# VectorE side work dealt out by kind of projection tile, and the key norm first in each RWKV pair, in a decoder step of retention and RWKV-7

## The chip, the cores and the metric

The kernel runs on one core of one Trainium2 chip. The metric is device time in microseconds (us) of one execution. The kernel before was timed three times. Engines are named as in the profile: PE is TensorE, PEld its weight loads, DVE is VectorE, ACT is ScalarE, POOL is GpSimd, SP is SyncE, which issues most of the transfers. SPq is SP's issuing queue. HBM is the chip's memory.

## The reference

One step of a hybrid decoder on 512 prompt rows and 8 sampled rows of 1024 values. One normalised input goes through one combined projection `w_in`. Branch A is retention (4 heads, keys of 256, values of 512), branch B is RWKV-7 (16 heads of 64). Each is gated, normalised and projected down; both are merged, projected out, and followed by an embedding gate and a last norm.

```
P = rmsnorm(x) @ w_in
q, k, v, g_a, sh, g_b, m_a, m_b = split(P)
# branch A, per head, chunks of 128 rows
inner = (q k^T) * dmask;  o = inner v + (q * q_dec) S;  S = chunk_dec * S + (k * k_dec)^T v
y_a = rmsnorm(o) * silu(g_a)
# branch B, per head of 64; z = sh mixed with the row before
w = decay(w0 + tanh(wl) @ w2);  a = sigmoid(a0 + al @ a2)
kk = k * k_k / |k * k_k|
S = S * w - (S kk) (a * kk)^T + v k'^T;  o_t = S r_t
y_b = groupnorm(o) * silu(g_b)
out = x + (sigmoid(m_a) * (y_a @ w_down_a) + sigmoid(m_b) * (y_b @ w_down_b)) @ w_out, ...
```

The 8 sampled rows take one step from stored states of both branches.

## The kernel before

**Products.** Nearly all work on PE is a *tile*: 128 columns of a weight against the 520 rows (512 and 8), in two halves of 256 and 264 rows (`HV`). A product of 32-bit values is three passes, high by high, high by low and low by high, so that a half is 24 matmuls (`mm_half`, L154). `weights` fetches a tile's weights on SP's queue (`raw`, 512 KB), ACT copies the high part (`whi`, L141), and DVE subtracts it to get the low part (`wlo`, L142). There are two buffers of `whi` and of `wlo`, so that PE waits for a `wlo` that comes late. The second of three passes, the one that reads `wlo`, comes early in each half.

**Order.** The Tile framework puts each engine's instructions into an order of its own, from the program's order, its dependences and durations that it assumes, before anything runs. Each engine then works through its list strictly in turn: an instruction that waits holds up all that stands behind it on that engine. `tc.issue_after` keeps what it encloses behind a given instruction. Reordering the program's text thus moves instructions on all engines.

**Stages.** First the input, its norm and transposes, and the shifted key tiles (to 120 us). Then come 8 RWKV pairs (to some 262 us): each is a generator `pair` that the loop at L556 to L575 steps through, with the projection tiles of two pairs further on (`filler`) between its steps. Then come four retention heads (L735 to L861, from 262 to 740 us). The RWKV chunks follow (740 to 945 us), then the last projections.

**In a pair.** Two pairs are under way at a time: the first two steps of one stand just ahead of the `g` products of the pair before it. The first step makes the low-rank products on PE (`pw`, L440 and L441: two halves for the decay, two for `a`), which ACT takes out of PSUM with a tanh (`sg` and `a`, L442); DVE sums them up (`cum`, L445) and ACT raises them (`Pm`, `iP`). The second step makes the key norm (`pn`, L457, two halves), which DVE takes out by `kkn` (L458), and then `KRS`, `b1`, `BK`, `km` on DVE. Later steps make the 16 products `g` (L498), which DVE masks (`GM`, L504); DVE's rescaling `BK` (L518); PE's transposes of `BK` (L523), that ACT takes out (`BKT`, L524); transposes of the values and the bonus `pb`. All of `pw`, `pn`, `g`, the transposes and `pb` take turns in three PSUM banks (`bank()`, tag "x"); one more bank takes the fourth `g`. The projections' halves have four banks of their own.

**In a head.** Key and query tiles with their rotation (`rope`: two tiles each; on DVE the products L751 to L753, the second of which goes to a buffer `s_` of which there is one), four value tiles, scores (`sc`, L787), the values' transposes (`vt`, L800; ACT takes `vhi`, DVE `vlo` L802), the sampled rows (`sampled`, L690), four gate tiles (`gs`, L823, ACT with Silu), in heads 2 and 3 also four tiles of branch B's gate (L828, O_GB), the outputs `o` (L838), their norms (`rsqrt`, chains of small DVE operations L172 to L180), the new states `st` (L849, through the buffer `s_` and a store on POOL's queue), the transposes `ot` and the products with the gates `gs` (L858).

**Side work.** DVE also has work that PE doesn't wait for until the chunks: `solve` (L608), 62 steps of two dependent operations on a buffer `M` (L614 and L616; 8 stores to `TTd` at the end), and `rwkv_sampled` (L634), 4 times 9 operations on a state that is loaded into the same buffer `M` when the stores have read it. `beside` (L663) strings both together with a pause between. `advance` (L671) deals them out: it adds a share of `WORK` to `due` and issues steps until what they cost (elements and 60 for each) has used it up. It is called behind each key, query, value and gate tile, 12 times in a head, always with the share 1/42; the pause is worth two shares.

Of the kernel before, what the change touches and what calls it, by code (L numbers as in the profile page):

```python
# [8 lines left out]
F32 = mybir.dt.float32  # L9
# [3 lines left out]
ALU = mybir.AluOpType  # L13
# [4 lines left out]
T, B8, NT = 512, 8, 520  # L18
HT = 256
D = 1024  # L20
KT = 8
# [3 lines left out]
H = 4  # L25
# [7 lines left out]
V_MU, V_W0, V_A0, V_KK, V_KA, V_RK, V_LW, V_LB, V_PG = 0, 25, 33, 41, 49, 57, 65, 73, 81  # L33
# [46 lines left out]
def body(tc, A, O, dbg=None, upto="Z"):  # L80
# [3 lines left out]
    act, dve, pe, sp, pool = nc.scalar, nc.vector, nc.tensor, nc.sync, nc.gpsimd  # L84
# [7 lines left out]
    with es:  # L92
# [15 lines left out]
        def bank(name="x", tag="x"):  # L108
            return px.tile([128, 512], F32, tag=tag, name=name)
# [18 lines left out]
        HV = ((0, 0, HT), (1, HT, NT))  # L128
# [33 lines left out]
        def proj(src, rhi, rlo, **kw):  # L162
            return mm([(*weights(src), 0, KT)], rhi, rlo, **kw)
# [33 lines left out]
        vcol = lambda o, i: vec[:, o + i:o + i + 1]  # L197
# [7 lines left out]
        def gate(c_, m, dst, fn, scale=1.0):  # L205
            g = gp.tile([128, NT], F32, tag="mg", name="mg", bufs=2)
            for (j, c0, c1), ps in zip(HV, proj(w_in[:, col(c_, m)], hhi, hlo)):
                act.activation(g[:, c0:c1], ps, fn, scale=scale)
            sp.dma_start(dst[m], g)
# [114 lines left out]
        pA = pA_.__enter__()  # L324
# [55 lines left out]
        zk = []  # L380
        pss = [bank("pss") for _ in range(2)]
        for p in range(NPAIR):
# [14 lines left out]
            if p == 2:  # L397
                gb = pA.tile([128, D], F32, tag="GM", name="gb")
# [18 lines left out]
        rns = pA.tile([128, NT], F32R, tag="zwa", name="rns", bufs=1)  # L417
# [6 lines left out]
        inh = pA.tile([128, NPAIR, 128], F32R, tag="inh", name="inh", bufs=1)  # L424
# [7 lines left out]
        SPL = 2  # L432
        def pair(p, zr, zv):
            cs = slice(p * 128, (p + 1) * 128)
            sg = pA.tile([128, NT], F32, tag="sgt", name="sg")
            a = pA.tile([128, NT], F32, tag="a", name="a")
            for dst, bi, u, w, wl in ((sg, p, W[0], Z[0], ZL[0]), (a, 8 + p, W[1], Z[1], ZL[1])):
# [13 lines left out]
            act.activation(iP, cum[:, 0:T], AF.Exp, scale=0.5 * E05)  # L451
            dve.tensor_copy(PC[:, p, :], Pm[:, :, C])
            yield
            kkn = pA.tile([128, NT], F32, tag="kkn", name="kkn")
            for j, c0, c1 in HV:
                pn = bank("pn")[:, 0:c1 - c0]
                pe.matmul(pn, inh[:, p, :], rns[:, c0:c1], start=True, stop=True)  # L457
                dve.scalar_tensor_tensor(kkn[:, c0:c1], zk[p][:, c0:c1], vcol(V_KK, p), pn, ALU.mult, ALU.mult)  # L458
            KRS = pA.tile([128, NCH, 128], F32, tag="KRS", name="KRS")
            k4 = KRS.rearrange("p (c e) (f t) -> p c (e f) t", e=2, f=2)  # L460
            P0 = Pm.rearrange("p (c e) t -> p c e t", e=2)
# [43 lines left out]
            for hh in range(2):  # L505
                hs_ = slice(64 * hh, 64 * hh + 64)
                GM = GMs[hh]
                h = 2 * p + hh
# [100 lines left out]
        def solve():  # L609
            for s in range(1, C - 1):  # L610
                n = C - 1 - s
                tm = pB.tile([128, 1024], F32, tag="tm", name="tm", bufs=1)
                tv = tm[:, 0:s * n].rearrange("p (i t) -> p i t", t=n)
                dve.tensor_tensor(tv, M[:, 0:s, s:s + 1].to_broadcast([128, s, n]),  # L614
                                  M[:, s:s + 1, s + 1:C].to_broadcast([128, s, n]), ALU.mult)
                dve.tensor_tensor(M[:, 0:s, s + 1:C], M[:, 0:s, s + 1:C], tv, ALU.add)  # L616
                yield s * n
            dve.memset(M.rearrange("p s t -> p (s t)")[:, 0::C + 1], 1.0)
            for c in range(NCH):
                sp.dma_start(TTd[c].rearrange("t h u -> h t u"), M[c * 16:(c + 1) * 16])  # L620
            yield 0
# [40 lines left out]

        def beside():  # L663
            yield from solve()
            yield 2 * WORK / 42
            yield from rwkv_sampled()

        extra = beside()
        due, WORK = 0.0, sum(s * (C - 1 - s) + 60 for s in range(1, C - 1)) + 36 * (HQ * C / 2 + 60)

        def advance(share=1.0 / 42):  # L671

            nonlocal due
            due += share * WORK
            with tc.issue_after(marks[1]):
                while due > 0:
                    w_ = next(extra, None)
                    if w_ is None:
                        break
                    due -= w_ + 60  # L680
# [54 lines left out]
        for h in range(H):  # L735
            roped = {}

            def rope(nm, c_):
                xx = rp.tile([128, 2, NT], F32, tag="rx", name="rx")
                for i in range(2):  # L740
                    x = xx[:, i, :]
                    for (j, c0, c1), ps in zip(HV, proj(w_in[:, col(c_, i)], hhi, hlo)):
                        act.activation(x[:, c0:c1], ps, AF.Copy)
                    advance()
                hi = pB.tile([128, 2, T], F32R, tag=nm + "hi", name=nm + "hi")
                lo = pB.tile([128, 2, T], F32R, tag=nm + "lo", name=nm + "lo")
                res = []
                for i, (u, w, op) in enumerate(((xx[:, 0], xx[:, 1], ALU.subtract), (xx[:, 1], xx[:, 0], ALU.add))):
                    m1 = pB.tile([128, NT], F32, tag=f"ro_{nm}", name="m1", bufs=2)
                    m2 = pB.tile([128, NT], F32, tag="s_", name="m2", bufs=1)  # L750
                    dve.tensor_tensor(m1, u, cos, ALU.mult)  # L751
                    dve.tensor_tensor(m2, w, sin, ALU.mult)
                    dve.tensor_tensor(m1, m1, m2, op)  # L753
                    act.activation(hi[:, i, :], m1[:, 0:T], AF.Copy)
                    dve.tensor_tensor(lo[:, i, :], m1[:, 0:T], hi[:, i, :], ALU.subtract)
                    act.activation((qs if nm == "q" else ks)[:, h, i, :], m1[:, T:NT], AF.Copy, scale=1.0 if nm == "q" else 1 / 16.0)
                    res.append(m1)
                roped[nm] = (hi, lo, res)

            def values():  # L760
                for i in range(4):
                    x = pB.tile([128, NT], F32, tag="vg", name="vT", bufs=4)
                    for (j, c0, c1), ps in zip(HV, proj(w_in[:, col(O_V + DV * h, i)], hhi, hlo)):
                        act.activation(x[:, c0:c1], ps, AF.Copy)
                    vT.append(x)
                    advance()

            vT = []
            if False:
# [12 lines left out]
            for jt in range(4):  # L782
# [3 lines left out]
                for x, (i, a_, b_) in enumerate(seq):  # L786
                    pe.matmul(ps[:, 0:n], a_[:, i, 128 * jt:128 * jt + 128], b_[:, i, 128 * jt:T],  # L787
                              start=(x == 0), stop=(x == 5))
# [31 lines left out]
            for i in range(4):  # L820
                g = pB.tile([128, NT], F32, tag="vg", name="gs", bufs=4)
                for (j, c0, c1), ps in zip(HV, proj(w_in[:, col(O_GA + DV * h, i)], hhi, hlo)):
                    act.activation(g[:, c0:c1], ps, AF.Silu)  # L823
                act.activation(gs8[:, 4 * h + i, :], g[:, T:NT], AF.Copy)
                gs.append(g)
                advance()
            for m in range(GBC[h], GBC[h + 1]):
                gate(O_GB, m, GBd, AF.Silu)  # L828

            oss = pB.tile([128, 4], F32, tag="oss", name="oss", bufs=2)  # L830
            ort = pB.tile([128, 4], F32, tag="ort", name="ort", bufs=2)
# [26 lines left out]
                dve.tensor_tensor(y, ps, y, ALU.mult)  # L858
                sp.dma_start(YAd[4 * h + i], y)
            sampled_out(h, po)  # L860
        advance(1.0)  # L861
        pR_.__exit__(None, None, None)
        pB_.__exit__(None, None, None)
        rp_.__exit__(None, None, None)
# [323 lines left out]
        for x in HV:  # L1188
            j = x[0]
# [48 lines left out]
```

## Time and profile before

| what | value |
|---|---|
| runs of the kernel before | 1121.35, 1121.46, 1123.13 us; median 1121.46 |
| the profiled execution | 1122.57 us |
| its span | 1120.8 us |
| its mean granted TensorE clock | 0.976 of full |
| PE busy | 1066.7 us, 95% of the span |
| DVE, ACT, POOL busy | 786.1, 508.1 and 63.0 us |
| read from HBM, written | 139.28 and 61.58 MB |
| chain that ended last | PE 79%, DMA 10%, DVE 6%, ACT 3% |

The span is what the profiler saw from the first to the last instruction; the execution's own time is 1.8 us longer. A busy share is an average over stages. Where one engine is busy nearly all the time, its idle stretches show what the others could give back, and each idle stretch is listed with the instruction that ended it. The granted clock is in shares of full speed: 1.00 is 2.4 GHz, 0.50 is 1.2 GHz.

### The profile page before, as it was taken

The page shows a single profiled execution, that of the slowest core. Times are in us where ns is not written, and L with a number is a line of the kernel's source. Part 1 is how long each engine was busy: PE and PEld are TensorE (multiplying, and loading weights), DVE is VectorE, ACT ScalarE, POOL GpSimd, SP SyncE. Part 2 cuts the span into 40 slices and gives each one's busy share as a digit, 9 for nine tenths or more (in the row PEclk, how much of TensorE's full clock was granted, in tenths as well). Part 3 has the DMA queues.
Part 4 walks back from the last instruction along what each step waited for, and adds up shares of the span by engine and source line. Part 5 has one row for each costly group of instructions (what it writes and reads, how often), then busy time and mean ns, then how long its engine had stood idle before and what let it go on. Part 6 is the DMA issues. An engine that isn't in the chain of part 4 may idle for free.

```text
span 1120.8 us, 22849 instructions
## 1 busy us (share of the span) xinstructions
PE 1066.7 (95%) x9324; PEld 1018.3 (91%) x9324; DVE 786.1 (70%) x1433; ACT 508.1 (45%) x1037; POOL 63.0 (6%) x98
## 2 busy tenths in 40 slices
PE   7999999999899989999999999999889799999996
PEld 6999998999898889889898998999889799999995
DVE  6647887883598999976695975245878564666775
ACT  6745644654544453373337343334432123434554
POOL 2000000000200200010011001010000100000000
PEclk8999999999999999999999999999999899999998
DMA  5632677798932942394667436489998458743322
GB/s 175 177 87 79 153 200 166 183 251 218 352 103 67 314 160 72 115 326 120 192 225 292 142 98 201 137 262 330 287 290 233 122 143 241 255 141 94 95 57 77
DMA packets 253659, 202.65 MB, mean 181 GB/s; under 512 B 59220, under 2 KB 220865, under 8 KB 252402
## 3 DMA queue, kind: packets, MB, share of 16 engines
q1 hardware_dynamic: 240146, 153.27, 47.6%
q0 software_dynamic: 13248, 47.65, 12.1%
q8 instruction: 73, 1.20, 0.4%
q14 instruction: 32, 0.26, 0.1%
q10 hardware_dynamic: 160, 0.27, 0.1%
HBM read 139.28 MB, written 61.58 MB: 179 GB/s over the span
## 4 chain that ended last, share of the span: by engine, by line
PE 79%; DMA 10%; DVE 6%; ACT 3%; issue 1%; SPq 0%; POOL 0%; DVEq 0%; POOLq 0%; ACTq 0%
PE ph L154 64%; DMA ya<-YAd 3%; PE o L838 3%; PE st L849 2%; PE g L498 2%; PE po L712 1%; DMA yb<-BNd 1%; DVE wlo L142 1%; ACT whi L141 1%; PE sc L787 1%; DMA YBd<-yb 1%; DMA raw<-in_w_in_dram 1%; DMA BKt<-BKd 1%; PE vb L704 1%; DMA xt<-in_x_prompt_dram 1%
## 5 line engine op out<-in xcount | busy, mean ns | idle before, releaser
L154 PE MATMUL ph<-hhi,whi 128*128 128x256 f32 (+2 forms) x1552 | 445.9, 288 | 5.0 <-ACT gs L823 2.4
L154 PE MATMUL ph<-hhi,wlo 128*128 128x256 f32 (+2 forms) x1552 | 442.5, 286 | 3.7 <-DVE wlo L142 3.7
L154 PE MATMUL ph<-hlo,whi 128*128 128x256 f32 (+2 forms) x1552 | 444.9, 287 | 0.3 <-DVE hlo L276 0.3
L154 PEld LDWEIGHTS ph<-hhi,whi 128*128 128x128 f32 x1552 | 295.1, 190 | 9.0 <-ACT gs L823 2.7
L154 PEld LDWEIGHTS ph<-hhi,wlo 128*128 128x128 f32 x1552 | 295.5, 191 | 7.1 <-DVE wlo L142 4.1
L154 PEld LDWEIGHTS ph<-hlo,whi 128*128 128x128 f32 x1552 | 295.4, 190 | 2.2 <-DVE hlo L276 1.0
L142 DVE TENSOR_TENSOR wlo<-raw,whi 128x1024 fp32r<-128x1024 f32 x135 | 165.0, 1223 | 105.6 <-ACT whi L141 104.4
L141 ACT ACTIVATE whi<-raw 128x1024 fp32r<-128x1024 f32 x135 | 142.9, 1059 | 210.6 <-PE ph L154 188.4
L154 PE MATMUL ph<-yahi,whi 128*128 128x256 f32 (+1 forms) x256 | 75.2, 299 | 4.4 <-ACT yahi L984 2.8
L154 PE MATMUL ph<-yalo,whi 128*128 128x256 f32 (+1 forms) x256 | 74.8, 295 | 0.5 <-DVE yalo L985 0.4
L154 PE MATMUL ph<-yahi,wlo 128*128 128x256 f32 (+1 forms) x256 | 74.0, 295 | 0.1
L614 DVE TENSOR_TENSOR tm<-M 128x62 f32<-128x62 f32 (+30 forms) x62 | 53.0, 854 | 10.6 <-DMA raw<-in_w_in_dram 10.0
L154 PEld LDWEIGHTS ph<-yahi,whi 128*128 128x128 f32 x256 | 50.3, 198 | 6.3 <-ACT yahi L984 3.8
L616 DVE TENSOR_TENSOR M<-M,tm 128x62 f32<-128x62 f32 (+30 forms) x62 | 52.9, 854 | 0.5
L154 PEld LDWEIGHTS ph<-yalo,whi 128*128 128x128 f32 x256 | 50.7, 198 | 1.4 <-DVE yalo L985 1.3
L154 PEld LDWEIGHTS ph<-yahi,wlo 128*128 128x128 f32 x256 | 50.1, 198 | 0.8 <-DVE wlo L142 0.6
L707 DVE SCALAR_TENSOR_TENSOR tS<-vb,ks,tS 128x512 f32<-128x512 f32 x64 | 43.9, 745 | 3.1 <-PE vb L704 3.1
L154 PE MATMUL ph<-yblo,whi 128*128 128x264 f32 (+1 forms) x128 | 37.1, 291 | 1.3 <-DVE yblo L1059 1.3
L154 PE MATMUL ph<-ybhi,whi 128*128 128x256 f32 (+1 forms) x128 | 36.8, 289 | 0.8 <-ACT ybhi L1058 0.8
L706 ACT ACTIVATE tS<-tS 128x512 f32<-128x512 f32 x64 | 35.1, 622 | 4.5 <-DMA tS<-in_state_ret_dram 4.3
L154 PE MATMUL ph<-ybhi,wlo 128*128 128x264 f32 (+1 forms) x128 | 36.6, 288 | 0.0
L154 PE MATMUL ph<-mglo,whi 128*128 128x264 f32 (+1 forms) x128 | 36.2, 283 | 0.0
(436 smaller groups left out, 1936.8 us busy)
## 6 DMA issues: line engine op xcount, KB each, us to landing
raw<-in_w_in_dram SPq DMA_DIRECT2D x97, 512.0 KB, 4.6
tS<-in_state_ret_dram POOLq DMA_DIRECT2D x16, 1024.0 KB, 8.4
out_dram<-tS POOLq DMA_DIRECT2D x16, 1024.0 KB, 7.8
KR<-KRd SPq DMA_DIRECT2D x8, 1024.0 KB
raw<-in_w_down_a_dram SPq DMA_DIRECT2D x16, 512.0 KB, 8.4
KRd<-KRS SPq DMA_DIRECT2D x16, 256.0 KB, 4.1
KRd<-GM SPq DMA_DIRECT2D x16, 256.0 KB, 3.2
YAd<-gs SPq DMA_DIRECT2D x16, 256.0 KB, 3.0
```

Source lines behind the costliest of these rows:

```text
L141: cp = act.activation(hi, raw, AF.Copy)
L142: sb = dve.tensor_tensor(lo, raw, hi, ALU.subtract)
L154: m_ = pe.matmul(ps[:, 0:c1 - c0], w[:, k, :], r[:, k0 + k, c0:c1], start=(x == 0), stop=(x == n_ - 1))
L498: ms = [pe.matmul(gs[2 * q + hh][:, c * 128:(c + 1) * 128], BK[hs_, 4 * q + c, :], KRS[hs_, 4 * q + c, :], start=True, stop=True) for q in ...
L614: dve.tensor_tensor(tv, M[:, 0:s, s:s + 1].to_broadcast([128, s, n]), M[:, s:s + 1, s + 1:C].to_broadcast([128, s, n]), ALU.mult)
L616: dve.tensor_tensor(M[:, 0:s, s + 1:C], M[:, 0:s, s + 1:C], tv, ALU.add)
L704: pe.matmul(vb, sel[:, 4 * g + b, :], vsr, start=True, stop=True)
L706: act.activation(S[:, b, :], S[:, b, :], AF.Copy, scale=GAM[h])
L707: last = dve.scalar_tensor_tensor(S[:, b, :], vb, ks[:, h, i, 4 * g + b:4 * g + b + 1], S[:, b, :], ALU.mult, ALU.add)
L712: m_ = pe.matmul(po[32 * b:32 * b + n_, :], qz[:, i, b, 32 * g:32 * g + n_], S[:, b, :], start=(n_ == 32), stop=(g == 1 and i == 1), skip_ ...
L838: pe.matmul(ps, a_[:, o_:o_ + 128], b_[:, jt, :], start=(x == 0), stop=(x == len(seq) - 1))
L849: pe.matmul(ps, a_[:, jt, 128 * i:128 * i + 128], b_[:, jt, :], start=(x == 0), stop=(x == 11))
```

## The change

The change has two parts.

In `pair`, the key-norm product `pn` and its evictions `kkn` are moved from the head of the second step to the head of the first, ahead of the low-rank products.

In the heads, `advance` takes the kind of the tile that was issued last. Its share is the kind's load over the sum of loads, `UNITS` (124): 1 for a key or query tile, 3.5 for a value tile, 1 for a gate tile, 3.5 for a tile of branch B's gate (where there was no call), and 3 behind the outputs at each head's end (where there was none either). Head 0's key and query tiles get no call. The pause between `solve` and `rwkv_sampled` is worth 6 of the 124. No instruction is added or removed on any engine; the whole change is one of order.

```diff
         def pair(p, zr, zv):
             cs = slice(p * 128, (p + 1) * 128)
+            kkn = pA.tile([128, NT], F32, tag="kkn", name="kkn")
+            for j, c0, c1 in HV:
+                pn = bank("pn")[:, 0:c1 - c0]
+                pe.matmul(pn, inh[:, p, :], rns[:, c0:c1], start=True, stop=True)
+                dve.scalar_tensor_tensor(kkn[:, c0:c1], zk[p][:, c0:c1], vcol(V_KK, p), pn, ALU.mult, ALU.mult)
             sg = pA.tile([128, NT], F32, tag="sgt", name="sg")
...
             dve.tensor_copy(PC[:, p, :], Pm[:, :, C])
             yield
-            kkn = pA.tile([128, NT], F32, tag="kkn", name="kkn")
-            for j, c0, c1 in HV:
-                pn = bank("pn")[:, 0:c1 - c0]
-                pe.matmul(pn, inh[:, p, :], rns[:, c0:c1], start=True, stop=True)
-                dve.scalar_tensor_tensor(kkn[:, c0:c1], zk[p][:, c0:c1], vcol(V_KK, p), pn, ALU.mult, ALU.mult)
...
         def beside():
             yield from solve()
-            yield 2 * WORK / 42
+            yield 6 / UNITS * WORK
             yield from rwkv_sampled()
...
-        def advance(share=1.0 / 42):
-
+        LOAD = dict(k=1, q=1, v=3.5, gate=1, out=3, gb=3.5)
+        UNITS = H * (4 + 4 * 3.5 + 4 + 3) - 4 + KT * 3.5
+
+        def advance(kind=None):
             nonlocal due
-            due += share * WORK
+            due += LOAD[kind] / UNITS * WORK if kind else WORK
...
-                    advance()
+                    if h:
+                        advance(nm)
...
-                    advance()
+                    advance("v")
...
-                advance()
+                advance("gate")
             for m in range(GBC[h], GBC[h + 1]):
                 gate(O_GB, m, GBd, AF.Silu)
+                advance("gb")
...
             sampled_out(h, po)
-        advance(1.0)
+            advance("out")
+        advance()
```

Three places show what this does to the order. The first is DVE at the start of head 0: `qz` is cleared for the sampled rows, `wlo` are the low parts of weights, `tm` and `M` are the solve's two operations, `m_` and `klo` belong to the rotation of the keys. Before:

```order
L692 MEMSET qz 128x272
L142 TENSOR_TENSOR wlo<-raw,whi 128x1024
L614 TENSOR_TENSOR tm<-M 128x62
L616 TENSOR_TENSOR M<-M,tm 128x62
L614 TENSOR_TENSOR tm<-M 128x122
L751 TENSOR_TENSOR m_3778<-rx,cos 128x520
L616 TENSOR_TENSOR M<-M,tm 128x2x61
L142 TENSOR_TENSOR wlo<-raw,whi 128x1024
```

And with the change:

```order
L696 MEMSET qz 128x272
L142 TENSOR_TENSOR wlo<-raw,whi 128x1024
L756 TENSOR_TENSOR m_3748<-rx,cos 128x520
L142 TENSOR_TENSOR wlo<-raw,whi 128x1024
L756 TENSOR_TENSOR m_3756<-rx,cos 128x520
L757 TENSOR_TENSOR m_3749<-rx,sin 128x520
L758 TENSOR_TENSOR m_3748<-m_3748,m_3749 128x520
L757 TENSOR_TENSOR m_3757<-rx,sin 128x520
L758 TENSOR_TENSOR m_3756<-m_3756,m_3757 128x520
L760 TENSOR_TENSOR klo<-m_3748,khi 128x512
L142 TENSOR_TENSOR wlo<-raw,whi 128x1024
L614 TENSOR_TENSOR tm<-M 128x62
```

The solve's first operation moved from behind the first of these weight tiles to behind the third, and behind the key's rotation.

The second place is DVE where head 0 ends and head 1 begins: L172 to L180 are the norms' small chains, `gs` the products with the gates, `M` and `tm` the solve again. Before:

```order
L178 TENSOR_TENSOR nt<-ort 128x4
L616 TENSOR_TENSOR M<-M,tm 128x30x33
L179 TENSOR_TENSOR nt<-nt,nv 128x4
L614 TENSOR_TENSOR tm<-M 128x992
L180 SCALAR_TENSOR_TENSOR ort<-nt,ort 128x4
L616 TENSOR_TENSOR M<-M,tm 128x31x32
```

And with the change:

```order
L178 TENSOR_TENSOR nt<-os_4743 128x1
L179 TENSOR_TENSOR nt<-nt,nv 128x1
L180 SCALAR_TENSOR_TENSOR os_4743<-nt,os_4743 128x1
L864 TENSOR_TENSOR gs<-ot,gs 128x512 x2
L142 TENSOR_TENSOR wlo<-raw,whi 128x1024
L614 TENSOR_TENSOR tm<-M 128x920
L756 TENSOR_TENSOR m_5033<-rx,cos 128x520
```

Before, each small operation of the norm stands behind one of the solve's large ones; now the two norms and two of the four products with the gates run through first.

The third place is DVE in the second RWKV pair, from its `kkn` to the rescaling of `BK` (L518) that PE's transposes read. `g`, `GM` and L518 are those of the pair before, all else is the second pair's. Before:

```order
L458 SCALAR_TENSOR_TENSOR kkn<-zk,vec,pn 128x256
L458 SCALAR_TENSOR_TENSOR kkn<-zk,vec,pn 128x264
L445 SCALAR_TENSOR_TENSOR cum<-reset,sg 128x520
L466 SCALAR_TENSOR_TENSOR b_1771<-a,kkn 128x520
L452 COPY PC<-Pm 128x8
L462 TENSOR_TENSOR KRS<-Pm,kkn 128x4x128
L463 TENSOR_TENSOR KRS<-Pm,zr 128x4x2x64
L504 TENSOR_TENSOR GM<-g,gmask 128x512 x2
L468 TENSOR_TENSOR BK<-b_1771,iP 128x8x64
L471 TENSOR_TENSOR km<-a,zk 128x520
L504 TENSOR_TENSOR GM<-g,gmask 128x512 x2
L518 TENSOR_TENSOR BK<-BK,Pm 128x1024
```

And with the change:

```order
L466 SCALAR_TENSOR_TENSOR b_1771<-a,kkn 128x520
L450 SCALAR_TENSOR_TENSOR cum<-reset,sg 128x520
L504 TENSOR_TENSOR GM<-g,gmask 128x512 x2
L471 TENSOR_TENSOR km<-a,zk 128x520
L457 COPY PC<-Pm 128x8
L462 TENSOR_TENSOR KRS<-Pm,kkn 128x4x128
L463 TENSOR_TENSOR KRS<-Pm,zr 128x4x2x64
L468 TENSOR_TENSOR BK<-b_1771,iP 128x8x64
L472 TENSOR_TENSOR BK<-km,iP 128x8x64
L474 SCALAR_TENSOR_TENSOR t_1779<-zr,vec,km 128x520
L504 TENSOR_TENSOR GM<-g,gmask 128x512 x2
L518 TENSOR_TENSOR BK<-BK,Pm 128x1024
```

`kkn` moved out of this stretch, ahead of it; the second `BK` product (L472) and L474 moved into it, ahead of the last two masks `GM` and of L518.

## Rows read from the trace of the kernel before

**Rows 1.** The page's first part: busy us, share, instructions.

```profile
PE 1066.7 (95%) x9324; PEld 1018.3 (91%) x9324; DVE 786.1 (70%) x1433; ACT 508.1 (45%) x1037; POOL 63.0 (6%) x98
```

**Rows 2.** Windows by stage: stretch, length, busy PE, PEld, DVE, ACT, POOL, PEclk, DMA share, GB/s.

```profile
120.00:262.00 142.00, 135.00 (x1170) 130.11 (x1169) 111.66 (x194) 75.58 (x166) 0.00 (x0) 0.98 0.76 188
293.00:740.00 447.00, 432.37 (x3277) 404.25 (x3277) 346.23 (x549) 203.91 (x414) 34.90 (x51) 0.98 0.55 177
740.00:945.00 205.00, 191.83 (x2414) 182.68 (x2412) 126.89 (x254) 63.32 (x93) 12.33 (x14) 0.97 0.81 240
```

**Rows 3.** Waits of PE, 262 to 740 us: total, times, longest (us).

```profile
PE vt L800 <- DVE vlo L802: 6.0, 3, 2.8
PE ph L154 <- DVE wlo L142: 3.2, 1, 3.2
PE ph L154 <- ACT gs L823: 2.4, 1, 2.4
PE ph L154 <- ACT vT L764: 1.9, 1, 1.9
PE ot L856 <- DVE gs L858: 1.1, 1, 1.1
```

**Rows 4.** Waits of PE, 120 to 262 us.

```profile
PE g L498 <- DVE kkn L458: 3.6, 5, 1.2
PE pn L457 <- ACT sg L442: 2.3, 2, 1.2
PE g L498 <- ACT a L442: 0.5, 1, 0.5
```

**Rows 5.** Windows: two behind waits, one undisturbed.

```profile
345.90:349.20 3.30, 3.30 (x18) 3.30 (x17) 2.18 (x3) 0.95 (x5) 0.00 (x0) 0.50 0.48 136
451.70:455.00 3.30, 3.30 (x16) 2.74 (x17) 3.30 (x7) 2.50 (x9) 0.00 (x0) 0.50 0.48 147
296.40:299.80 3.40, 3.40 (x28) 3.40 (x29) 3.40 (x8) 1.33 (x3) 0.00 (x0) 1.00 0.86 331
```

**Rows 6.** Timeline, 281 to 296 us, SP's queue and DVE: start, busy, instruction [wait before].

```profile
281.91 1.95 SPq L607 DMA_DIRECT2D M<-XTd  x1
...
293.60 0.22 DVE L614 TENSOR_TENSOR tm<-M 128x62 f32<-128x62 f32 x1 [9.97 <-DMA raw<-in_w_in_dram]
...
295.13 1.22 DVE L142 TENSOR_TENSOR wlo<-raw,whi 128x1024 fp32r<-128x1024 f32 x1
```

**Rows 7.** Timeline, ACT, end of head 0's values.

```profile
343.70 1.28 ACT L823 ACT_TABLE_LOAD   x1
345.00 1.23 ACT L823 ACTIVATE gs<-ph 128x256 f32<-128x256 f32 x4
```

**Rows 8.** Timeline, DVE, between heads 0 and 1.

```profile
394.96 0.16 DVE L180 SCALAR_TENSOR_TENSOR ort<-nt,ort 128x4 f32<-128x4 f32 x1
395.08 1.19 DVE L616 TENSOR_TENSOR M<-M,tm 128x992 f32<-128x992 f32 x1
```

**Rows 9.** Timeline, 521 to 549 us, DVE, SP's and POOL's queues.

```profile
521.11 0.27 DVE L616 TENSOR_TENSOR M<-M,tm 128x62 f32<-128x62 f32 x1
...
521.41 14.40 SPq L620 DMA_DIRECT2D TTd<-M  x8
...
541.08 2.12 POOL L637 DMA_DIRECT2D S__6439<-in_state_rwkv_dram  x4 [38.98 <-DMA raw<-in_w_in_dram]
...
547.66 1.22 DVE L642 TENSOR_TENSOR rT<-S__6439,sv 128x1024 f32<-128x1024 f32 x1 [6.04 <-DMA S__6439<-in_state_rwkv_dram]
```

**Rows 10.** Timeline, 137 to 150 us, a pair: PE, ACT and DVE.

```profile
137.59 0.28 PE L440 MATMUL pw<-Z,W 128*128 128x264 f32 x1
...
137.65 1.06 ACT L141 ACTIVATE whi<-raw 128x1024 fp32r<-128x1024 f32 x1
...
141.28 3.55 PE L498 MATMUL g<-KRS,BK 64*128 64x128 f32 x30 [0.46 <-DVE kkn L458]
...
148.38 1.21 DVE L518 TENSOR_TENSOR BK<-BK,Pm 128x1024 f32<-128x1024 f32 x1
```

## The prediction

> **What bounds the kernel now.** I read the page's first part first: PE is busy for 95% of the span, and DVE, second, for 70% [rows 1]. So time can come only out of the stretches in which PE stands still or runs at its lower clock, and DVE matters where PE waits for it. The windows by stage [rows 2] tell where these are: the pairs leave PE idle for 7 us of 142, the heads for 15 of 447, the chunk stage for 13 of 205. The change reorders work in the first two, and hardly moves PE's order in the third. The waits of PE then name what ended each gap. In the heads five lines hold 14.6 us [rows 3], in the pairs three hold 6.4 [rows 4]. The timeline around each gap, last, tells what the waiting instruction stood behind.
>
> A gap of PE costs more than itself. Behind four of the heads' gaps the granted clock of a stretch of some 3.4 us is 0.50, the lower level of 1.2 GHz: 18 and 16 matmuls start in 3.3 us there, against 28 in 3.4 us at 2.4 GHz [rows 5]. At 0.121 us for a matmul at the upper level (3.40/28) these 9 to 11 missing ones are 1.1 to 1.3 us; I take 1.3 for such a fall. The gaps that had one are 2.4 us and longer or two short ones in a row, 1.9 behind 1.1 in the heads and 0.46 behind 1.12 in two pairs. The 3.2 us gap had none [rows 3, 5]. So a fall is likely behind a gap over 2, and not sure.
>
> **The heads, wait by wait.** No instruction is added or removed; each term is a wait that goes, stays or comes.
>
> The wait of 3.2 us for `wlo`. The solve's first operation needs `M`, whose load is issued at 281.91; it starts at 293.60, having waited on DVE for 9.97 us [rows 6]. DVE goes in order, and the `wlo` behind it starts at 295.13. In the new order this operation stands behind two more weight tiles. A half is 24 matmuls, so a tile takes 2 x 24 x 0.121 = 5.8 us; two more put it 11.6 us later, beyond the landing. Gain 3.2; `M` need be ready only then, and the late thing next would be the solve itself, 62 steps for which nobody waits before the chunks.
>
> The wait of 2.4 us for `gs`. In head 0 ACT loads a table for Silu (1.28 us) ahead of the first gate eviction, which starts at 345.00 [rows 7]. ACT's order is unchanged there. It stays, with its fall: 3.7.
>
> The waits of 1.1 and 1.9 us between heads 0 and 1. The norm is 24 operations of some 0.16 us, and one of the solve's of 1.19 us stands behind each of most of them [rows 8]; so `gs`, the rotated keys and `vT` come late, all behind the same chain. In the new order they run together. Gain 3.0 and the fall, 4.3.
>
> The three waits for `vlo`, 6.0 us. Two are in head 1, where 16 transposes `vt` stood together on PE and the solve's operations of about 1 us stood between the evictions. Now the transposes stand 4, 4 and 8 apart with projections between, but PE then reaches the first gate sooner than ACT can take it out: I put 1.5 there, less than head 0's 2.4 as no table is loaded, and half a chance of a fall, 2.2 in all. The third is in head 2: the last solve step ends at 521.4, the eight stores of `M` hold SP's queue for 14.40 us, the loads into the same buffer are issued at 541.08, and the first sampled product starts at 547.66 after 6.04 us of waiting, with a `vlo` behind it [rows 9]. This handover takes 26.3 us. In the new order it falls between heads 2 and 3, and that product stands behind three more weight tiles' low parts, about 29 us after the last solve step by 5.8 us a tile and what heads do between. That is just enough. For heads 2 and 3 I leave 0.4 and 0.8 (a short burst of transposes in each; bounds 0 and head 1's former 3.3).
>
> Before: 14.6 and four falls of 1.3, 19.8. After: 3.7 + 2.2 + 0.4 + 0.8 = 7.1. Gain 12.7. Bounds: 19.8 if all waits go; 4 if a gate wait as head 0's comes in each head (below).
>
> **The pairs.** All products but the projections share three banks. Before, `pn` waited for the third bank back, that of `sg`, whose eviction stands on ACT behind a `whi` of 1.06 us [rows 4, 10]; `g` then waited for `kkn`. In the new order `pn` goes first and DVE takes it early, but `g` now waits for ACT's last evictions, behind the same `whi`. The first product begins at 137.59 and most of `g` 3.7 us later [rows 10]; by the six evictions in their new order I get 2.75 later. For two of the pairs that is a gap of 1.1 where 1.6 were. For two more it is the other way, 1.5 for 1.2, for the others 0.7 together. Second, DVE's rescaling (L518) now stands behind two more operations. Before, it started at 148.38 and ended 12.0 us after the first product [rows 10]; I get 12.4. PE, with `g` earlier and not slowed, would reach the transposes at 2.75 + 2.45 + 48 x 0.121 = 11.0, so a new gap of some 1.4 to 1.7; I take 1.7 in the two pairs that gain. Bounds: nothing, if PE is as late as before, and 1.7 in all eight. After: 2 x 2.8 + 2 x 1.5 + 0.7 = 9.3 against 6.4; the two falls of before stay two. Loss 2.9.
>
> The gap of about one length that returns pair after pair [rows 4] is what the Trainium skill (Perfetto Trace Analysis, Optimization Strategy) calls consistent bubbles, which can mean that there is no SBUF or PSUM for the next tile. By that rule the order of taking banks would not matter while their number stays three. The trace agrees as to the banks in the two waits for `sg` alone; the five for `kkn` are for data.
>
> **The rest.** Stores and loads are the same ones in the same amounts; the chunk stage's 13 us [rows 2] are kept. If the state's loads and stores of branch B, now later by most of a head, met the chunk stage's transfers, that would cost; its DMA share of 0.81 speaks for a little of that, and the new shares end by the last head. I take 0.
>
> **Sum.** -12.7 + 2.9 = -9.8. The profiled execution took 1122.57, which is 1.1 above the median; so 1121.46 - 9.8 = 1111.7. What a measurement of this kernel can tell from no change is about 0.2%, 2.2 us: below 1119.2 is faster, above 1123.7 slower.
>
> **The rivals.**
>
> Pairs unchanged (chance 0.16). The banks bind whichever product comes first, and the pairs stay at 6.4: 1121.46 - 12.7 = 1108.8. For it: the banks' number. Against it: most waits of before name DVE.
>
> Pairs gain (0.10). L518 is in time, and most waits for `kkn` go: another 5 us, 1103.8. For it: `kkn` really is early in the new order.
>
> The handover takes some back (0.13). The state loads come later than I think, DVE waits on them as at 547.66 and a `wlo` or a store's buffer (`s_`, used by the rotation of head 3) stands behind: up to the 6.04 us of [rows 9]: 1117.7.
>
> ACT's gate evictions bind in every head (0.09). With the `vlo` waits gone PE meets `gs` in all four as in head 0, 4 x 3.7 = 14.8 instead of 19.8: -5.0 + 2.9, 1119.4, no change to be told.
>
> Slower (0.10): DVE's rescaling comes late in all eight pairs. Each gets 1.7 us and a fall of the clock; two had one, so 8 x 1.7 + 6 x 1.3 = 21.4, less the heads' 12.7: +8.7, 1130.2. It decides from about 1.9 us a pair on, where 8 times that is more than the heads' gain and 2.2. For it: a 1.12 us gap with 0.46 behind it did bring a fall, so a second gap in each pair can. Against it: only the pairs in which PE comes sooner can wait longer.
>
> That the change does nothing is shut out by the orders: `M` moves by two weight tiles, the norm's chain is closed.
>
> **The numbers.** My forecast has 0.42; it has the two larger of the known waits gone. The range reaches from just below the gaining pairs (1103) to above the unchanged case (1121), and leaves out the slower case, some of the gaining one's lower half and tails. Faster: 0.42 + 0.16 + 0.10 + 0.13 is 0.81, less a tail of the handover case, 0.80. Same 0.10, slower 0.10.
>
> **What would show it.** Among PE's waits from 262 to 740 us the 3.2 for `wlo` at 293 should be gone, `gs` in head 0 should be there with 2.4, `vlo` should be down from 6.0 to 1 or 2, and the window of the heads shorter by 12 to 13 us. In the pairs, waits for `kkn` should give way to waits for ACT's `a` or `sg`, and a wait of the transposes (L523) for L518 of 1 to 2 us should appear. If that wait stands in all the pairs, or if clock falls number over ten, the slower case holds. The forecast is wrong if a `wlo` or `vlo` waits again behind a state load near 600 us, or if the heads lose less than 8 us of gaps.

## The result, and the profile after

| | before | after |
|---|---|---|
| median | 1122.30 us (4 runs, 1121.35 to 1124.30) | 1104.74 us (4 runs, 1101.37 to 1107.18) |
| ratio, 95% interval | | 0.9839 (0.9809 to 0.9869) |
| profiled execution, its span | 1122.57, 1120.8 | 1104.80, 1103.0 |

The change makes the kernel faster by some 17.6 us; the interval of the ratio allows 14.7 to 21.4. The forecast was 9.8 us. The time lies within its range, but 7 us below the 1111.7 that it had in the middle.

The page's first part has PE busy for 14 us less than before [rows 1], with the same instructions:

```profile
PE 1052.5 (95%) x9324; PEld 1005.7 (91%) x9324; DVE 786.7 (71%) x1433; ACT 506.8 (46%) x1037; POOL 63.1 (6%) x98
```

That is the sign of a higher mean clock rather than of shorter waits. To see it by stage I added up, over the trace, PE's idle stretches above 0.1 us from its first instruction on and, in brackets, the time at the granted clock of 0.50; one stretch of that is called a fall, and most last 3.4 us. The stages are cut at 105 us, at 262 us, 8 us behind the last `st` product, and ahead of the final transposes (`xo`):

| kernel | start | pairs | heads | chunks and behind |
|---|---|---|---|---|
| before | 3.5 (6.8) | 6.9 (6.8) | 14.6 (13.7) | 14.4 (17.1) |
| after | 4.0 (6.8) | 8.8 (0) | 9.8 (3.4) | 13.4 (3.4) |

The idle time fell by 3.5 us of the profiled executions' 17.8, the time at 1.2 GHz by 30.8 us. If the other 14.3 us are all the clock's, they are 0.46 us for each us at the lower clock, or 1.6 for a fall of 3.4 us. This is an estimate, and an average over the stages.

PE's waits from 262 to 740 us of the kernel after, which answer to [rows 3] (the columns are the same):

```profile
PE ph L154 <- ACT gs L828: 4.0, 3, 2.4
PE vt L805 <- DVE vlo L807: 2.8, 1, 2.8
PE ph L154 <- DVE wlo L142: 2.5, 2, 2.3
```

The 3.2 us for `wlo` at 293 and the two waits between heads 0 and 1 are gone. The `gs` wait of 2.4 stands as before. The `wlo` wait of 2.3 is a new one, at 624 us. The one `vlo` wait left is a burst of 16 transposes in head 3.

And from 120 to 262 us, which answer to [rows 4]:

```profile
PE g L523 <- DVE Pm L452: 3.1, 2, 1.6
PE g L498 <- ACT sg L447: 2.6, 2, 1.3
PE pw L445 <- ACT sg L447: 2.0, 3, 0.8
PE pw L445 <- DVE kkn L439: 0.6, 1, 0.6
```

The waits for `kkn`'s data are gone; waits for banks that ACT (`sg`) or DVE (`kkn`) empties, and of the transposes (L523) behind DVE, have come in their place.

Up to the end of the heads the forecast's sum is met (by errors that cancel, see below); the rest lies behind it. The last `st` products, by the view of that tile (count, duration, first and last start), before:

```profile
L849 PE MATMUL st<-vlo,dhi x32: 390/392/404, 388.2 to 730.6; 128*128 128x512 f32 x32
```

and after:

```profile
L855 PE MATMUL st<-vlo,dhi x32: 387/392/404, 379.2 to 720.3; 128*128 128x512 f32 x32
```

They come 10.3 us earlier; the end of the program comes 17.8 us earlier. The chunk stage, at which the forecast put nothing, gave 7.5. By the table 1.0 of this is idle time; 13.7 us less at the lower clock are an estimated 6.3.

### The profile page after: what moved, and what is told of

Same layout as the page of the kernel before. It is cut to its first block, busy times and chain, and to the rows that moved or that the text cites. A ratio compares the mean times of both kernels' runs of the same rounds, so it can differ in the third digit from the quotient of the medians.

```text
span 1103.0 us, 22852 instructions
## 1 busy us (share of the span) xinstructions
PE 1052.5 (95%) x9324; PEld 1005.7 (91%) x9324; DVE 786.7 (71%) x1433; ACT 506.8 (46%) x1037; POOL 63.1 (6%) x98
## 4 chain that ended last, share of the span: by engine, by line
PE 61%; issue 15%; DMA 13%; DVE 6%; ACT 3%; POOL 1%; SPq 1%; DVEq 0%; POOLq 0%; ACTq 0%
PE ph L154 50%; DMA out_dram<-tS 2%; DMA ya<-YAd 2%; DMA tS<-in_state_ret_dram 2%; PE g L498 1%; PE o L844 1%; DMA raw<-in_w_in_dram 1%; PE st L855 1%; DMA out_dram<-st 1%; DMA yb<-BNd 1%; DMA YBd<-yb 1%; DMA BKt<-BKd 1%; ACT whi L141 1%; DVE wlo L142 1%; PE sc L792 1%
## 5 line engine op out<-in xcount | busy, mean ns | idle before, releaser
L154 PE MATMUL ph<-yahi,whi 128*128 128x256 f32 (+1 forms) x256 | 72.9, 291 | 4.4 <-ACT yahi L991 3.3
L154 PE MATMUL ph<-yahi,wlo 128*128 128x264 f32 (+1 forms) x256 | 72.0, 288 | 0.7 <-DVE wlo L142 0.6
L154 PE MATMUL ph<-mghi,whi 128*128 128x264 f32 (+1 forms) x128 | 36.1, 282 | 0.0
```

Source lines behind the costliest of these rows:

```text
L154: m_ = pe.matmul(ps[:, 0:c1 - c0], w[:, k, :], r[:, k0 + k, c0:c1], start=(x == 0), stop=(x == n_ - 1))
```

## The experiments

Idle times and the brackets behind them are counted as in the table above.

### The two parts apart

`heads_only` puts `pn` and `kkn` back where they were and keeps the rest; `pairs_only` moves them and keeps the old dealing.

```diff
             cs = slice(p * 128, (p + 1) * 128)
-            kkn = pA.tile([128, NT], F32, tag="kkn", name="kkn")
...
             yield
+            kkn = pA.tile([128, NT], F32, tag="kkn", name="kkn")
...
             KRS = pA.tile([128, NCH, 128], F32, tag="KRS", name="KRS")
```

This is `heads_only` against the change; `pairs_only` is the same with the signs turned round, against the kernel before.

> The dealing by kind alone, with the pairs as before. Theory 1 (each part is worth what its stage shows): the heads give about 8.6 us, the pairs stay as before with waits of 6.4 us for kkn and sg and two clock falls near 141 and 182 us; the chunk stage gives its 7.5 us too, since its order comes with the heads': about 1106, some 1.7 over the full change. Theory 2 (what the full change gained in the chunk stage came of transfers and clock falls that happened to meet otherwise, not of its order): only the heads' part is sure, 1113, anything from 1106 to 1114. The 3.2 us wait for wlo at 293 is gone under both.

> The key norm first, alone, with the side work dealt out as before. Theory 1: 1.7 us faster than before, about 1120: waits in the pairs rise from 6.9 to about 8.7 us, with the transposes' wait for L518 of 1.5 us in two pairs, and the two clock falls there are gone. The heads show before's waits of 14.6 us and four falls. Theory 2: the pairs' own waits are 1.8 us longer, and whether the clock falls depends on more than the gap's place: 1119 to 1124, the chunk stage anywhere within its 7.5 us.

`heads_only`: 1105.52 us, ratio 0.9865 (0.9825 to 0.9904). `pairs_only`: 1123.43 us, 1.0022 (0.9988 to 1.0056). The dealing carries all of the gain that can be told; the key norm first is worth nothing that can be. In its profile (1127.88 us, next to the slowest of its twelve runs, which took 1117.84 to 1128.14) `pairs_only` has the pairs of the change (8.8 idle, no fall) and waits in the heads that are longer than before's:

```profile
PE vt L800 <- DVE vlo L802: 7.1, 3, 3.9
PE ph L154 <- DVE wlo L142: 6.7, 1, 6.7
```

The second is the wait of 3.2 at 293 [rows 3]: here the load of `M` was issued 2.7 us later than in [rows 6], and the solve's first operation started 3.2 us later. So with the old dealing this wait also moves with whatever comes ahead; the new one takes it away. `pairs_only` missed theory 1's 1120 and lies in theory 2's range; in the profiled execution this wait and a start that was some 1.4 us longer idle are a part of why.

### Does a gap bring its fall with it?

24 more transposes of the identity at the start move the whole program in time.

```diff
-WARM = 20
+WARM = 44
```

> The kernel before with 24 more transposes of the identity ahead of the first real work (44 for 20; they compute nothing), so that all later work has the same order and starts up to 3 us later. Theory 1 (a gap of a given length has its fall): the same gaps have the same falls, at 141, 182, 346, 418, 452, 551, 834, 871, 889 and 947 us plus the shift, and the time grows by 0 to 3 us. Theory 2 (a fall also depends on when the gap comes): the same gaps, but some falls go and others come; the time lies between 4 us less and 6 us more than before.

> The changed kernel with the same 24 more transposes at the start. Theory 1: falls behind the waits at 338 and 858 us alone, as in the changed kernel, and 0 to 3 us more. Theory 2: the gaps of 1.5 us and more at 149, 188, 624, 661 and 791 us, which had no fall, get some: up to 6 us more.

`before_shift`: 1120.41 us, ratio 0.9998 (0.9970 to 1.0025). From the pairs on its order on PE and DVE is that of the kernel before, but for a few projections in one place. It runs some 0.6 us earlier in the first pair and 1.3 to 2.6 us later in the heads. The first windows below are of the kernel before, behind the gaps of 1.12 and 0.46 us in a pair, and behind its longest chunk gap:

```profile
141.10:144.40 3.30, 3.12 (x28) 3.12 (x29) 3.19 (x7) 1.80 (x5) 0.00 (x0) 0.50 0.85 264
...
888.70:895.40 6.70, 5.71 (x29) 5.49 (x31) 5.26 (x12) 0.00 (x0) 1.11 (x2) 0.50 0.46 147
```

and this one is of `before_shift`, behind the same gaps of the same lengths:

```profile
140.70:144.10 3.40, 3.40 (x42) 3.28 (x43) 3.30 (x6) 2.15 (x6) 0.00 (x0) 1.00 0.97 297
```

The fall is not there. The same holds in the second pair that had one. Of the ten falls that theory 1 lists, those at 346, 418, 452, 551, 834 and 889 came back behind the same waits; 141, 182, 871 and 947 did not, though 141, 182 and 947 have their gaps as before, and a new one came at 293, in a wait for `wlo` that is now 4.3 us long. Theory 1 is out: whether a gap is followed by a fall depends on more than its length. What a pair saves then shows up as another wait. PE's timeline of `before_shift` (start, length, what, wait before), the first line from the first of the two pairs, the second from the second:

```profile
140.63 2.05 PE L498 MATMUL g<-KRS,BK 64*128 64x128 f32 x30 [0.46 <-DVE kkn L458]
...
189.46 1.06 PE L523 MATMUL g<-ident,BK 128*128 128x128 f32 x8 [1.74 <-DVE Pm L447]
```

The 30 products `g` take 2.05 us, not the 3.55 of [rows 10]; PE reaches the transposes earlier and waits for DVE there, 1.74 us in the second pair (0.2 in the kernel before) and 0.34 in the first (none before). So part of what a fall costs is only moved. The eight kernels with the change's order in the pairs show it best (after, `pairs_only`, `even`, `early_solve`, `st_sp`, `st_own`, `silu_early`, `best_a`). Five have no fall there and are idle for 8.8 us, three have one and are idle for 7.1 or 7.2. From the first `pw` to the last `pb` all eight take 151.1 to 151.2 us. There a fall and the wait for L518 are two forms of one loss.

`after_shift`: 1101.10 us, 0.9840 (0.9789 to 0.9891). It got falls at 659, 788 and 925 us that the change did not have, and its profiled execution is 4.3 us faster all the same. Here the order did move: in two pairs the transposes of `BK` stand further back, and the waits for L523 and for `sg` at `g` are gone from the list, so that the pairs idle for 4.2 us where the change has 8.8. From the first `pw` to the last `pb` they take 147.4 us, where the change takes 151.1. This run therefore says nothing clean on the falls, but it shows that the pairs' waits go with the place of these transposes, with the same three banks.

### Beside which tile, and how early

`even` gives value and gate tiles the same share, `early_solve` gives head 0's key and query tiles theirs back:

```diff
-        LOAD = dict(k=1, q=1, v=3.5, gate=1, out=3, gb=3.5)
+        LOAD = dict(k=1, q=1, v=2.25, gate=2.25, out=3, gb=3.5)
```

```diff
-                    if h:
-                        advance(nm)
+                    advance(nm)
...
-        UNITS = H * (4 + 4 * 3.5 + 4 + 3) - 4 + KT * 3.5
+        UNITS = H * (4 + 4 * 3.5 + 4 + 3) + KT * 3.5
```

> The changed kernel with the same share for a value and a gate tile, 2.25 each, so that each head gets the same amount as in the change but the kind of these tiles doesn't matter. Theory 1 (it counts how much side work a head gets, and when it starts and is handed over, not beside which tile): 1101 to 1109, PE's idle time in the heads 6 to 10 us. Theory 2 (the kind counts: side work beside gates delays evictions and norms): idle time in the heads 5 us more than the change's 9.8, 1110 or more.

> The changed kernel with head 0's key and query tiles getting shares again, so that the solve's first operation stands behind the first weight tile once more. Theory 1: PE's wait for wlo near 290 us is back, 3.2 to 6.7 us, some with a clock fall: 1107 to 1112. Theory 2 (by now M lands in time, or DVE has slack): no wait over 0.5 us there, 1102 to 1106.

`even`: 1100.47 us, 0.9802 (0.9751 to 0.9853), idle 6.3 in the heads. Theory 1 holds, if 0.5 us below its range: at these shares, with the same amount for each head, it makes no loss that can be told whether the side work stands beside value or gate tiles.

`early_solve`: 1113.59 us, 0.9927 (0.9903 to 0.9951), half of the gain lost and 1.6 us above theory 1's range. Its wait of PE for `wlo`, and the window behind it:

```profile
PE ph L154 <- DVE wlo L142: 4.8, 1, 4.8
```

```profile
295.50:302.20 6.70, 5.17 (x24) 5.17 (x25) 6.70 (x14) 2.66 (x7) 0.98 (x2) 0.50 0.95 352
```

4.8 us of wait and 6.8 us at the lower clock are an estimated 8 us. That settles the first term of the heads: the four calls that head 0 leaves out are what removes this wait. It is not the whole of the loss. The profiled execution is 8.9 us longer than the change's; by idle time and 0.46 us for each us at the lower clock, the heads cost 5.1 more (11.8 (10.2) against 9.8 (3.4), although head 3's new wait of 2.3 is not there) and the chunk stage 5.0 more.

`early_solve` also tells what the chunk stage gained. From about 740 us on its order on PE, DVE and ACT is, instruction by instruction, that of the kernel before. PE's largest wait from 740 to 945 us is, before, in `early_solve` and after:

```profile
PE gt L902 <- DVE yb L905: 6.2, 2, 5.2
```

```profile
PE gt L908 <- DVE yb L911: 5.0, 2, 4.6
```

```profile
PE gt L909 <- DVE yb L912: 4.0, 2, 2.8
```

The second of each is the wait of PE's transposes of the chunks' outputs (`gt`) for a bank that DVE empties once `yb` has been loaded behind a store. It is 4.6 to 5.2 us in all four kernels with the old order of this stage (before, `before_shift`, `pairs_only`, `early_solve`) and at most 1.2 in the five whose order there is the change's but for small shifts (after, `after_shift`, `heads_only`, `st_sp`, `silu_early`). Their chunk columns are 14.4 (17.1), 14.4 (10.2), 15.7 (13.7) and 13.7 (13.7) against 13.4 (3.4), 11.3 (10.2), 9.4 (6.8), 11.2 (3.4) and 10.3 (3.4). At 0.46 us for each us at the lower clock the old order costs 19 to 22 us there and the change's 12 to 16. So the gain comes with the order, though neither part of the change touches that code. One difference can be named. It is where DVE makes the sum `gva` for the norm that stands ahead of this store; before and after:

```profile
870.64 1.21 DVE L888 TENSOR_REDUCE gva<-gsq 128x16 f32<-128x1024 f32 x1
```

```profile
855.48 1.22 DVE L895 TENSOR_REDUCE gva<-gsq 128x16 f32<-128x1024 f32 x1 [0.46 <-ACT gsq L893]
```

Before, it runs behind the `yb` operations that DVE starts at 870.10 once a load has landed; after, it runs ahead of them, while DVE waits for that load until 859.98. From the start of these `yb` operations to the store's issue it is 6.8 to 7.4 us in the four kernels with the old order, and 4.8 to 5.3 in all others, `even` too. That is an estimated 2 of the 4 us of wait. The rest of the gain is mostly time at the lower clock, which varies within either order. `even` has a third order, no long `gt` wait, but 17.1 us at the lower clock, and costs as much as the old order; why its falls are so many stays open.

### The handover in head 3, and the first gate

The new wait of 2.3 us at 624 us. DVE and POOL's queue in the kernel after:

```profile
611.78 2.12 POOL L637 DMA_DIRECT2D S__7645<-in_state_rwkv_dram  x4 [18.15 <-DMA YAd<-gs]
613.89 0.55 POOL L858 DMA_DIRECT2D out_dram<-st  x1
```

```profile
619.65 1.23 DVE L642 TENSOR_TENSOR rT<-S__7645,sv 128x1024 f32<-128x1024 f32 x1 [4.92 <-DMA S__7645<-in_state_rwkv_dram]
620.80 0.69 DVE L756 TENSOR_TENSOR m<-rx,cos 128x520 f32<-128x520 f32 x1
624.71 0.70 DVE L757 TENSOR_TENSOR m<-rx,sin 128x520 f32<-128x520 f32 x1 [3.23 <-DMA out_dram<-st]
625.33 1.22 DVE L142 TENSOR_TENSOR wlo<-raw,whi 128x1024 fp32r<-128x1024 f32 x1
```

DVE waits twice: for the state, then for the store of head 2's second `st`, which stands on POOL's queue behind the four state loads and shares the buffer `s_` with the rotation (L757). The store lands at 624.69, 10.8 us after its issue. The `wlo` comes last.

`st_sp`, `st_own` and `silu_early`, each against the change (the Silu's result is not used):

```diff
-                pool.dma_start(O[2][0, 0, h, 128 * i:128 * i + 128, :], st)
+                (sp if h == 2 else pool).dma_start(O[2][0, 0, h, 128 * i:128 * i + 128, :], st)
```

```diff
-                st = pB.tile([128, DV], F32, tag="s_", name="st", bufs=1)
+                st = pB.tile([128, DV], F32, tag=("ihi", "ilo")[i], name="st")
```

```diff
                     if h:
                         advance(nm)
+                if h == 0 and nm == 'q':
+                    act.activation(warm, xx[:, 1, NT - 1:NT], AF.Silu)
```

> The changed kernel with the stores of head 2's new state on SP's queue, not on POOL's behind the loads of branch B's state. Theory 1 (head 3's rotation waits for the buffer s_ until that store has landed): PE's wait of 2.3 us for wlo at 624 goes, and with it the burst of 16 value transposes is drawn apart; 2 to 4 us less than the change, 1101 to 1103. Theory 2 (DVE waits for the state loads themselves, 4.9 us at 615): the wait at 624 stays over 1.5 us and nothing is gained.

> The changed kernel with the new state's two parts in the buffers of the scores' low and high parts (free by then) instead of in s_, so that head 3's rotation waits for no store. Theory 1 (the shared buffer s_ is what holds DVE at the start of head 3): PE's wait for wlo near 620 us is under 0.5, 2 to 3 us less than the change: 1101 to 1103. Theory 2 (DVE then waits for the loads of branch B's state instead): the wait stays at 1 to 2 us.

> The changed kernel with one Silu of a single column behind head 0's query tile (its result is not used), so that ACT loads the table for Silu there and not ahead of the first gate. Theory 1 (the load's 1.28 us are part of the 2.43 us that PE waits for the first gate): the wait falls to 1.0 to 1.3 us and the clock fall behind it may go: 1 to 3 us less, 1102 to 1104. Theory 2 (the two value evictions and the high weights ahead of it set the wait): still over 2 us.

`st_sp`: 1102.97 us, 0.9827 (0.9787 to 0.9867). A miss, though the time is in theory 1's range: the wait did not go, it grew to 3.9 us. On SP's queue the first of the two stores stood behind the solve's eight stores (issued at 603.32, not 593.07), the second, which waits for it, was issued at 610.32, landed at 620.18, and DVE still waited for it:

```profile
620.21 0.70 DVE L757 TENSOR_TENSOR m<-rx,sin 128x520 f32<-128x520 f32 x1 [7.81 <-DMA out_dram<-st]
```

DVE does wait for the store, but another queue was no remedy. `st_own`, which takes the shared buffer away, gives 1097.21 us, 0.9783 (0.9741 to 0.9825), below the 1101 to 1103 expected, with 4.8 us idle in the heads; the burst of transposes in head 3 is drawn apart too:

```profile
PE ph L154 <- ACT gs L828: 3.9, 3, 2.4
PE ph L154 <- DVE wlo L142: 0.5, 1, 0.5
PE kt L819 <- DVE vlo L807: 0.4, 1, 0.4
```

`silu_early`: 1097.71 us, 0.9796 (0.9751 to 0.9840), below the 1102 to 1104 expected. The first gate's wait fell from 2.43 to 1.01 us and had no fall behind it, so the table's load was part of it, as theory 1 had it. The order on PE and DVE is that of the change, so the two executions (1096.98 and 1104.80) can be compared place by place. At head 0's first `vs`, just ahead of the first gate, this one is 0.3 us ahead, at the first `st`, behind the gate, 3.2, at the last `st` 5.5 and at the end 7.8. So the table is worth some 3 of the 7 us. The handover's wait of PE went too, though the shared buffer is still there and DVE still waited 3.80 us for the store: it landed at 617.91, 6.8 us earlier than in the change, and PE came by only some 4 us earlier. The same is seen in `after_shift` (longest wait of PE for `wlo` 0.3). So the shared buffer makes this wait possible, and how early the solve's handover runs decides whether PE feels it.

### Together

`best_a` joins `even`, `st_own` and `silu_early`; `best_b` adds the 24 transposes for the other order of the pairs.

> Together: equal shares for value and gate tiles, the Silu table loaded early, and the new state in buffers of its own. If the three gains add up (4 for even, 7 for the table by their medians, 1 to 2 for the buffers): 1093 to 1096. If what the parts gained is mostly that clock falls went otherwise: 1096 to 1102, with the heads' idle time at 4 to 6 us all the same.

> The same with 24 more transposes at the start, with which the framework gives the pairs another order (the transposes of BK stand further behind): PE's idle time in the pairs 4.2 us as in the run with the later start, for 7 to 9: 3 to 5 us less than the kernel of the run beside it, 1089 to 1093. The rival: the pairs' gain is lost again by a clock that falls elsewhere: the same time within 2 us.

`best_a`: 1094.30 us, 0.9763 (0.9732 to 0.9794), idle 2.3 in the heads. `best_b`: 1091.30 us, 0.9735 (0.9698 to 0.9773), idle 4.2 in the pairs and 3.7 in the heads, and two falls in all between the start and the end. Its waits from 120 to 740 us, the three largest:

```profile
PE pw L445 <- ACT sg L447: 2.4, 5, 0.7
PE ph L154 <- DVE wlo L142: 1.5, 2, 0.8
PE pw L445 <- DVE kkn L439: 1.4, 4, 0.6
```

Both beat both kernels; the intervals of the two overlap, so the last step's 3 us are not shown by the times, only the pairs' 4.6 us less of idle time by the trace. The three gains do not add up: by medians below 1104.74 they were 4.3 (`even`), 7.5 (`st_own`) and 7.0 (`silu_early`), and 10.4 came with `best_a`. Its time is in the expectation's range for gains that add up only because that counted 1 to 2 for the buffers. Each of the three took the handover's wait away or cut it, which can be gained only once.

## Why the prediction was right, point by point

The direction and the range were right. The size came about partly by luck: 7.5 us come from a stage at which the prediction put nothing, and by two of its own signs its account of the heads was wrong. A `wlo` did wait behind the state loads, at 624 us, and the heads lost 4.8 us of gaps (14.6 to 9.8), where it had named less than 8 as a sign against it.

- **`wlo` at 293, gain 3.2.** Right: the wait is gone, and `early_solve`, which undoes this part, brings it back with 4.8.
- **The first gate, 2.4 and a fall.** Right: 2.43, and the only fall in the heads. Two windows of the kernel after, behind this gate's wait and behind the handover's 2.3 us:

```profile
342.10:345.40 3.30, 3.30 (x18) 3.30 (x17) 1.76 (x3) 0.38 (x1) 0.00 (x0) 0.50 0.08 25
626.70:630.00 3.30, 3.30 (x28) 3.30 (x29) 3.30 (x5) 0.55 (x2) 0.00 (x0) 1.00 0.57 158
```

- **Between heads 0 and 1, 3.0 and a fall.** Right: no wait there is left. No run tests the norm's chain by itself as the cause. (The two norms are 13 operations each, 26 and not 24; nothing rests on it.)
- **Heads 1 to 3.** Head 1's gate 1.2 for 1.5, head 2's 0.4 for 0.4. Head 3 was mis-sized: 0.8 forecast, 5.0 measured, of which 2.3 are the handover (the third rival named it, with the buffer `s_` in it, at up to 6) and 2.8 the burst of `vt`. The step that failed is "That is just enough": the store behind the state loads was the one that came last.
- **The pairs, a loss of 2.9.** The gaps came out as worked: 8.8 idle for 9.3, `g` 3.05 us behind the first product for 2.75, the transposes' waits 1.6 and 1.5 for 1.7. But "the two falls of before stay two" failed: there were none, so that 1.9 us more of idle time stand against an estimated 3.1 of clock, a gain of 1.2. The prediction also weighed, from the page that it names (the Trainium skill, Perfetto Trace Analysis, Optimization Strategy: consistent bubbles can mean that SBUF or PSUM is short), that the pairs would stay as they are while there are three banks. The waits themselves moved, from data to banks, and with three banks `after_shift` has 4.2 us of them where the change has 8.8; but the time of `pairs_only` cannot be told from before's.
- **The falls.** A fall was put at 1.3 us. The profiles' balance gives 1.6 on average; the first gate, where `silu_early` saves 2.9 us with a wait 1.4 shorter and its fall, agrees, and in the change's pairs a fall costs nothing that can be seen. They were forecast gap by gap; `before_shift` shows that a gap's length does not tell.
- **"The chunk stage's 13 us are kept. I take 0."** This is the step that failed most, by 7.5 us: a wait of 5.2 us for `yb` became 1.2 (another grew, so that idle time fell by 1.0 in all), and the time at the lower clock fell from 17.1 to 3.4 us. The reasons given were that the change hardly moves PE's order there and that the loads and stores are the same in amount. But the order did move, on DVE too (`gva`), and the runs show that it counts.

The sum up to the end of the heads, 9.8 forecast and 10.3 measured, is luck in part, as two errors cancel. By idle time and the estimate of 0.46, the heads gave 9.5 for 12.7, mostly as head 3 waited for 4 us more; the pairs gave 1.2 where a loss of 2.9 was forecast; the start took 0.5.

## What to carry to other kernels

Ask of side work on an in-order engine two things before how evenly it is spread: is its input there when its first operation reaches the head of the list, and does a transfer that it sets off share a queue or a buffer with something the main work waits for. Then add the clock: here a gap of 1 to 3 us was followed by a fall in one run and by none in another, and a fall cost from nothing to some 1.6 us, so forecast falls as a chance per gap, not by the gap's length alone. And where a framework orders the instructions, compare the order of every stage, also those whose code is untouched.

## What had not been expected of the hardware

One and the same program spread wide: of 23 executions of the kernel before, timed beside the first four experiments, 22 took 1111.25 to 1126.64 us and one 1128.04. Only one execution of each kernel was profiled, but kernels with the same order in a stretch suggest what such a spread is made of: falls that come or stay away behind the same gaps, and transfers that land earlier or later. Up to the first `pw`, for one, `silu_early` has the change's order and takes 104.5 us where the change takes 106.4; the change has 6.8 us at the lower clock there and `silu_early` none. So 0.2% was too fine a bound for single runs of this kernel. The other surprise was that eight stores of one buffer hold SP's queue for 14.40 us before [rows 9], 17.48 after and 14.57 to 15.19 in `after_shift`, `st_sp` and `silu_early`; in `st_sp` the store put behind them on that queue was issued only when they were through.
